# Alternating the two head halves of the Gram products, and grouping attention scores by term, in a two-layer trunk step

## The chip, the cores and the metric

The kernel runs on one core of a Trainium2 chip. The metric is the device time of one execution in microseconds. The kernel before takes 3819.39 us (median of 3 runs, 3814.24 to 3825.59). The engines of the core are named as in the profile: PE is the matmul engine (TensorE), PEld its weight loads, DVE VectorE, ACT ScalarE, POOL GpSimd, and SP the engine that issues the DMAs.

## The reference

One inference step of a two-layer trunk over 128 context tokens and 512 latent tokens, width 2048, all in float32. Every layer is a modulated RMSNorm, a mixer, and a gated residual.

Layer 0 has eight differential-attention heads and eight multi-head-latent-attention (MLA) heads. A latent query reads 512 latent keys and 256 context keys in one softmax; a context query reads the 128 context keys. What matters here is the scores:

```python
# differential head, for each of its two score maps c
s = einsum('bqhcd,bkhcd->bhcqk', q, k_all) * 64 ** -0.5
# MLA head: two products are added
s = (einsum('bqhd,bkhd->bhqk', qn, k_nope) + einsum('bqhd,bkd->bhqk', qp, kpe_all)) * 192 ** -0.5
```

Layer 1 is a bidirectional RWKV-7 scan over 32 heads of width 64:

```python
sa = einsum('bhij,bhj->bhi', s, -kk_t)
s = s * w_t[:, :, None, :] + sa[..., None] * (kk_t * a_t)[:, :, None, :] + v_t[..., None] * k_t[:, :, None, :]
y_t = einsum('bhij,bhj->bhi', s, r_t)
```

The outputs are both token streams after a final RMSNorm, the new caches and the new scan states.

## The kernel before, in words

Activations lie transposed, with the channels on the partitions and the 640 tokens along the free axis. The large projections run in `project_steps` (L111): a weight chunk is split into a high part (ACT, L100) and a low part (POOL, L101), and each product is taken as three matmuls of 320 columns per token half (L126, tile `pj`). One step of this generator is one pair of matmuls. TensorE's program order is written out by hand: around every small piece of attention or scan the program calls `fill(w)`, which issues `w` times a quota of projection steps. The other engines' order comes from a scheduler with priorities.

**Attention scores (`scores`, L370).** For 128 queries the keys stand in one or two segments: 512 latent keys and 256 context keys for latent queries, one segment of 128 for context queries. Scores are a sum of terms. In a differential head there are two: a stacked high-precision product with 128 rows (`KA`), and a low-order correction that reads only the 64 partitions of its own score map (`KL`). In an MLA head there are three: the 128-row product (`kn`), the rope product with 128 rows (`kpeh`), and its correction with 64 rows (`kpel`). The two segments go to two PSUM banks of one tile `S`. The loop takes the segments one after the other, and all terms inside a segment. `S` has one buffer; DVE's maximum (L362) and ACT's exponential (L365) read it before the next scores may be written.

**The scan.** It runs in 32 units, two for each tile of 128 channels, and a tile holds two heads: head half 0 on partitions 0 to 63, half 1 on 64 to 127. A unit covers ten chunks of 64 tokens. The stages of several units overlap: while `stage_c` of unit n steps through the recurrence, earlier stages prepare the units n + 1 and n + 2. After `stage_c`, the list `P2` says in which order the rest of the preparation is done and how much projection work follows each step. `stage_a2` (L1104) of unit n + 2 is last in that list.

`stage_a2` makes the Gram products: for every chunk and each head half one fp32 matmul with 64 rows, 128 stationary columns and 128 moving columns (L1114), `BK` against `AR`. Four chunks of one half fill one PSUM bank, and DVE multiplies the bank with the triangular mask into `GG` (L1117). The PSUM pool `pg` that these banks come from has two buffers, which the stages `a1`, `kk`, `bk`, `pre`, `gn` and `bonus` use too. The stage is a generator with six steps: chunks 0 to 3 of half 0, then of half 1, chunks 4 to 7 of each, chunks 8 and 9 of each. `stage_a3` later sends `GG` through a DRAM buffer (`Ld`) and inverts its diagonal blocks; `stage_c` and `stage_pre` read `GG` as well.

Of the kernel before, what the change touches and what calls it, by code (L numbers as in the profile page):

```python
# [53 lines left out]
def kernel(  # L54
# [189 lines left out]
    with tc.tile_pool(name="x0", bufs=1, side="right") as xp0, \  # L244
# [11 lines left out]
        pss = [pt[:, 512 - HT:512], pt[:, 512:512 + HT]]  # L256
# [63 lines left out]
    with l0:  # L320
# [47 lines left out]
            return P, r  # L368

        def scores(S, terms, qa, segs):  # L370
            so = 0
            for (ka, kb) in segs:
                for i, (q, k) in enumerate(terms):
                    pe.matmul(S[:, so:so + kb - ka], q[:, qa:qa + 128], k[:, ka:kb],  # L374
                              start=(i == 0), stop=(i == len(terms) - 1))
                so += kb - ka

        def stack_q(QA, q, c):
            me, ot = slice(64 * c, 64 * c + 64), slice(64 - 64 * c, 128 - 64 * c)
# [151 lines left out]
        def s_part(H, t):  # L531
            qa, segs, kts = QT[t]
            n = 128 * len(kts)
            for c, terms in enumerate(H.terms):
                S = pS.tile([128, 1024], F32, tag="S", name="S")
                scores(S, terms, qa, segs)
                with tc.high_priority(offset=HP0):
                    P, r = softmax(S, n, f"P{c}", pools["dif"] if c else at)
                    if c == 0:
                        H.P = P  # L540
                        dve.tensor_scalar(out=P[:, 0:n], in0=P[:, 0:n], scalar1=r, scalar2=None, op0=ALU.mult)
                    else:
                        dve.tensor_tensor(out=r, in0=r, in1=nlam, op=ALU.mult)
                        dve.scalar_tensor_tensor(out=H.P[:, 0:n], in0=P[:, 0:n], scalar=r, in1=H.P[:, 0:n],
                                                 op0=ALU.mult, op1=ALU.add)
                yield
# [50 lines left out]
        def fill(w):  # L597
            quota[0] += w * quota[1]
            while quota[0] >= 1.0:
                quota[0] -= 1.0  # L600
                next(work[0], None)
# [236 lines left out]
    with ExitStack() as l1:  # L838
# [39 lines left out]
        def pg_tile(name):  # L878
            return pg.tile([128, 512], F32, tag="pg", name=name)
# [116 lines left out]
        def need(f, i):  # L996
            while i < 16 and (f, i) not in done:
                next(work[0])
# [105 lines left out]
        def stage_a2(i, u):  # L1104
            un = units[(i, u)]
            AR, BK = un.AR, un.BK
            GG = un.GG = u1.tile([128, NCH, 2, 128], F32, tag="GG", name="GG", bufs=2)
            for c in range(0, NCH, 4):
                n = min(4, NCH - c)
                for h in range(2):  # L1110
                    hs = slice(64 * h, 64 * h + 64)
                    ps = pg_tile("gram")
                    for j in range(n):
                        pe.matmul(ps[:, j * 128:(j + 1) * 128],  # L1114
                                  BK[hs, c + j, :, :].rearrange("p a t -> p (a t)"),
                                  AR[hs, c + j, :, :].rearrange("p a t -> p (a t)"), start=True, stop=True)
                    dve.tensor_tensor(  # L1117
                        out=GG[:, c:c + n, h, :], in0=ps[:, 0:n * 128].rearrange("p (j t) -> p j t", t=128),
                        in1=maskg.rearrange("p (o t) -> p o t", o=1).to_broadcast([128, n, 128]), op=ALU.mult)
                    yield  # L1120

        def stage_a3(i, u):
            un = units[(i, u)]
# [328 lines left out]
        def kk_of(n):  # L1452
            if n < len(seq) and seq[n][1] == 0:
                return stage_kk(seq[n][0])
            return iter(())

        def of(stage, n):
            return stage(*seq[n]) if n < len(seq) else iter(())

        def all_(*gens):  # L1460
            for g in gens:
                for _ in g:
                    pass

        def urgent(g):
            while True:
                with tc.high_priority(offset=HP):
                    try:
                        v = next(g)
                    except StopIteration:  # L1470
                        return
                yield v
# [8 lines left out]
                next(work[0], None)  # L1481

        CW = (3, 3, 2, 3)
        P2 = (('inv', 1), ('bk', 2), ('inv', 2), ('bk', 1), ('pre', 2), ('inv', 2), ('bonus', 1), ('bk', 1), ('inv', 2), ('pre', 2), ('bonus', 2), ('pre', 2), ('pre', 2), ('a2', 0), ('a2', 2), ('a2', 1), ('a2', 2), ('a2', 1), ('a2', 4))
        W2 = sum(w for _, w in P2)

        def step(g):
            next(g, None)

        def unit(n):  # L1490
# [23 lines left out]
            all_(sub, a1, gn, kk, of(stage_e, n + 2))  # L1514
            quota[1] = max(0.0, (total - w1) / W2)
            gens = dict(inv=inv, bk=of(stage_bk, n + 1), a2=of(stage_a2, n + 2), pre=of(stage_pre, n + 1), bonus=bonus)
            for k, w in P2:
                step(gens[k])
# [3 lines left out]
        def script(gens, items):  # L1522
            for k, w in items:
                step(gens[k])
                fill(w)
            all_(*gens.values())

        def prologue():
            quota[1] = 1.0
            need(proj_k, 0)  # L1530
            script(dict(kk=kk_of(0), a1=of(stage_a1, 0)),
                   (("a1", 9), ("a1", 9), ("kk", 9), ("kk", 7), ("a1", 7), ("kk", 5), ("a1", 0)))
            need(proj_r, 0)
            all_(of(stage_e, 0))
            fill(36)
            a1, bk = of(stage_a1, 1), of(stage_bk, 0)
            a2 = of(stage_a2, 0)
            for g, w in ((a2, 2), (a2, 2), (a1, 6), (a2, 2), (a2, 2), (a1, 6), (a2, 2), (a2, 2)):
                step(g)
                fill(w)  # L1540
            all_(a2, of(stage_a3, 0))
            for g, w in ((bk, 6), (bk, 6), (a1, 8), (bk, 6)):
                step(g)
                fill(w)
            all_(a1, bk)
            need(proj_v, 0)
            all_(of(stage_e, 1))
            of(stage_v, 0)
            script(dict(pre=of(stage_pre, 0), inv=urgent(of(stage_inv, 0)), a2=of(stage_a2, 1)),
                   (("pre", 6), ("pre", 32), ("inv", 3), ("a2", 3), ("inv", 3), ("a2", 3), ("a2", 3), ("inv", 3),  # L1550
                    ("a2", 3), ("pre", 3), ("inv", 3), ("a2", 3), ("pre", 3), ("a2", 3)))
            need(proj_r, 1)

        with tc.manual_schedule(engines={mybir.EngineType.PE}):
            prologue()
            for n in range(30):
                unit(n)
            unit(30)
            e2.release()
            ysp.append(tc.alloc_tile_pool(name="ysp", bufs=2, side="right"))  # L1560
            free_slots()
            unit(31)
            pc.release()
            pj3 = ctx.enter_context(tc.tile_pool(name="pj3", bufs=1, space=PSUM))
            gn = stage_gn(15, 1)
            step(gn)
            all_(work[0])
            all_(gn)
            stage_end(15, 1)
            y1_tile(15)  # L1570
            begun.append(out_begin(2, pj3, w_o1, y1hi, y1lo, 0))
            all_(interleaved([begun[2][1]], 3))
# [119 lines left out]
```

## Time and profile before

| what | before |
|---|---|
| median of 3 runs | 3819.39 us (3814.24 to 3825.59) |
| profiled execution | 3822.71 us, of which its span is 3820.9 us |
| mean granted TensorE clock | 0.979 |
| PE busy | 3607.5 us, 34176 matmul passes |
| DVE, ACT, POOL busy | 2203.8, 1607.6, 1193.5 us |
| MLA heads | about 230 to 625 us |
| differential heads | about 640 to 1280 us |
| Gram products (L1114) | 1628.6 to 3492.5 us, 1280 passes, 183.8 us busy |

The span runs from the first to the last instruction of the profiled execution. An fp32 matmul stands in the trace as two passes, each with a weight load (PEld) of its own; a matmul on the rounded type of the projections is one pass. A row gives an instruction's start, duration, engine, line, operation, and output and inputs by name; `64*128 64x128` means 64 rows and 128 stationary columns, and 64 partitions by 128 moving columns. The ends of matmuls are modelled and overlap the next one, so distances between starts say more than durations. "idle before" is the time in which the engine had nothing running ahead of a group, with what ended it.

### The profile page before, as it was taken

What the parts mean: (1) busy time and instruction counts of PE and PEld (TensorE: products, weight loads), DVE (VectorE), ACT (ScalarE), POOL (GpSimd) and SP (SyncE); (2) the same over time, 40 slices, a digit from 0 to 9 for tenths busy, and PEclk for the clock granted to TensorE, in tenths of its full rate; (3) what the DMA queues carried; (4) which work ended last, traced back from release to release, by engine and by line L of the source; (5) the groups of instructions that cost most, each with busy time, mean ns of one, the idle gap of its engine ahead of it and who ended that gap; (6) DMA issues with size and microseconds to landing.
All of it is one profiled execution on the core that took longest, in us unless ns stands there. A gap on an engine that the chain in (4) does not pass through costs nothing. (4 is left out here: it accounts for less than half of the span.)

```text
span 3820.9 us, 83259 instructions
## 1 busy us (share of the span) xinstructions
PE 3607.5 (94%) x34176; PEld 3121.5 (82%) x34176; DVE 2203.8 (58%) x4232; ACT 1607.6 (42%) x3310; POOL 1193.5 (31%) x1094
## 2 busy tenths in 40 slices
PE   8999999999999899999999999999999999999998
PEld 4778889888888798888777878878878787787898
DVE  3346655666567683555666566656666666666402
ACT  3244443444444323534444444434444444445422
POOL 1222122222222345433232232323323332232444
PEclk9999999999999999989999999999999999999999
DMA  8723333333334464322222222222222222223534
GB/s 296 233 68 106 113 91 109 104 101 106 104 103 131 147 206 142 91 64 56 71 60 62 59 61 71 60 62 57 66 69 60 67 59 65 67 65 85 164 99 141
DMA packets 388462, 376.18 MB, mean 98 GB/s; under 512 B 200496, under 2 KB 242416, under 8 KB 388080
## 3 DMA queue, kind: packets, MB, share of 16 engines
q1 hardware_dynamic: 388080, 370.86, 33.5%
q8 instruction: 268, 4.39, 0.5%
q14 instruction: 114, 0.93, 0.1%
HBM read 328.51 MB, written 42.24 MB: 97 GB/s over the span
## 5 line engine op out<-in xcount | busy, mean ns | idle before, releaser
L101 POOL TENSOR_TENSOR wlo<-raw,whi 128x512 fp32r<-128x512 f32 (+1 forms) x628 | 854.9, 1362 | 2164.9 <-PE pj L126 1303.2
L126 PE MATMUL pj<-h0hi,wlo 128*128 128x320 f32 x4448 | 1092.5, 324 | 18.7 <-POOL wlo L101 18.7
L126 PE MATMUL pj<-h0hi,whi 128*128 128x320 f32 x4448 | 1091.5, 324 | 4.5 <-DVE gt L951 3.1
L126 PE MATMUL pj<-h0lo,whi 128*128 128x320 f32 x4448 | 1083.8, 323 | 2.0 <-DVE h0lo L816 1.2
L126 PEld LDWEIGHTS pj<-h0hi,wlo 128*128 128x128 f32 x4448 | 748.0, 191 | 53.9 <-POOL wlo L101 22.4
L126 PEld LDWEIGHTS pj<-h0hi,whi 128*128 128x128 f32 x4448 | 747.7, 192 | 37.9 <-ACT whi L100 3.9
L126 PEld LDWEIGHTS pj<-h0lo,whi 128*128 128x128 f32 x4448 | 751.2, 191 | 29.4 <-DVE h0lo L816 1.5
L100 ACT ACTIVATE whi<-raw 128x512 fp32r<-128x512 f32 (+1 forms) x628 | 390.7, 623 | 793.0 <-PE pj L126 491.5
L198 DVE SCALAR_TENSOR_TENSOR aacc<-araw,scs,aacc 128x512 f32<-128x512 f32 x480 | 405.2, 892 | 17.8 <-DMA araw<-in_dram 16.8
L362 DVE TENSOR_REDUCE nm<-S 128x1 f32<-128x768 f32 (+1 forms) x120 | 98.4, 820 | 280.6 <-PE S L374 280.5
L1117 DVE TENSOR_TENSOR GG<-gram,con 128x512 f32<-128x512 f32 (+1 forms) x192 | 113.6, 599 | 145.2 <-PE gram L1114 144.2
L1114 PE MATMUL gram<-AR,BK 64*128 64x128 f32 x1280 | 183.8, 293 | 10.4 <-DVE GG L1117 5.2
L1114 PEld LDWEIGHTS gram<-AR,BK 64*128 64x128 f32 x1280 | 151.3, 192 | 44.2 <-issue 20.1
L722 DVE SCALAR_TENSOR_TENSOR x<-pj,mod,xr 128x512 f32<-128x512 f32 (+2 forms) x68 | 33.2, 524 | 248.7 <-PE pj L126 243.2
L365 ACT ACTIVATE P<-S,nm 128x768 f32<-128x768 f32 (+1 forms) x120 | 95.0, 792 | 175.7 <-DVE nm L362 175.5
L1302 ACT ACTIVATE Yn<-CC 128x128 f32<-128x128 f32 x160 | 44.3, 277 | 224.1 <-DVE rhs L1332 213.4
L1347 DVE COPY UV<-CC 64x128 f32<-64x128 f32 x160 | 47.1, 295 | 124.7 <-ACT UV L1346 123.1
L1054 PE MATMUL plo<-lr,lw 96*128 96x320 f32 x256 | 104.0, 488 | 6.6 <-DMA lr<-lorad 6.4
L1346 ACT ACTIVATE UV<-CC 64x128 f32<-64x128 f32 x160 | 43.1, 269 | 150.2 <-PE CC L1344 149.7
L564 PE MATMUL po<-PT,vt 128*128 128x128 f32 x800 | 103.2, 276 | 0.1
L564 PEld LDWEIGHTS po<-PT,vt 128*128 128x128 f32 x800 | 97.9, 191 | 4.2 <-issue 2.5
L1056 ACT ACTIVATE tmp<-plo,vecs 128x320 f32<-128x320 f32 x128 | 67.5, 527 | 66.1 <-PE plo L1054 66.0
(338 smaller groups left out, 5401.1 us busy)
## 6 DMA issues: line engine op xcount, KB each, us to landing
raw<-in_dram SPq DMA_DIRECT2D x612, 256.0 KB
araw<-in_dram SPq DMA_DIRECT2D x384, 256.0 KB
lr<-lorad SPq DMA_DIRECT2D x128, 120.0 KB
Ld<-GG SPq DMA_DIRECT2D x64, 160.0 KB
lw<-in_dram SPq DMA_DIRECT2D x128, 48.0 KB
x<-in_dram SPq DMA_DIRECT2D x16, 320.0 KB
xr<-in_dram SPq DMA_DIRECT2D x16, 320.0 KB
DD<-Xd SPq DMA_DIRECT2D x32, 160.0 KB
```

Of the source, the lines that this page charges most:

```text
L100: act.activation(out=hi, in_=src, func=AF.Copy)
L101: (lo_eng or pool).tensor_tensor(out=lo, in0=src, in1=rf(hi), op=ALU.subtract)
L126: pe.matmul(p[:n, 0:b - a], w, x[:, kk ^ flip, a:b], start=(kk == order[0] and i == 0), stop=(kk == order[-1] + kc - 1 and i == 2))
L198: dve.scalar_tensor_tensor(out=acc[:, s], in0=raw, scalar=scs[:, k, s:s + 1], in1=acc[:, s], op0=ALU.mult, op1=ALU.add)
L362: dve.tensor_reduce(out=nm, in_=S[:, 0:nk], axis=AX.X, op=ALU.max, negate=True)
L365: act.activation(out=P[:, 0:nk], in_=S[:, 0:nk], func=AF.Exp, bias=nm, accum_out=l)
L564: pe.matmul(po[:, 0:128], H.vt[:, kt, :], PT[:, j, :], start=(j == 0), stop=(j == n - 1))
L1054: pe.matmul(ps[:, 0:HT], lw, lo, start=True, stop=True)
L1056: act.activation(out=hv(tmp, z, ca, cb), in_=c3(ps[:, 0:HT]), func=AF.Exp, scale=-1.0, bias=nw0[:, bcol:bcol + 1])
L1114: pe.matmul(ps[:, j * 128:(j + 1) * 128], BK[hs, c + j, :, :].rearrange("p a t -> p (a t)"), AR[hs, c + j, :, :].rearrange("p a t -> p (a ...
L1117: dve.tensor_tensor(out=GG[:, c:c + n, h, :], in0=ps[:, 0:n * 128].rearrange("p (j t) -> p j t", t=128), in1=maskg.rearrange("p (o t) -> p ...
L1347: dve.tensor_copy(out=UV[64:128, cgs[1], :], in_=pu[1][64:128])
```

## The change

Three things are edited. In `scores` the two loops change places: the outer loop runs over the terms and the inner one over the key segments. In `stage_a2` both banks are taken at once, the matmuls of the two head halves alternate between them, and both masked copies follow; the generator has three steps instead of six. The three lists that call its steps are rewritten for three steps, with the same total of fill weights.

```diff
         def scores(S, terms, qa, segs):
-            so = 0
-            for (ka, kb) in segs:
-                for i, (q, k) in enumerate(terms):
+            for i, (q, k) in enumerate(terms):
+                so = 0
+                for ka, kb in segs:
                     pe.matmul(S[:, so:so + kb - ka], q[:, qa:qa + 128], k[:, ka:kb],
                               start=(i == 0), stop=(i == len(terms) - 1))
-                so += kb - ka
+                    so += kb - ka
...
             for c in range(0, NCH, 4):
                 n = min(4, NCH - c)
-                for h in range(2):
-                    hs = slice(64 * h, 64 * h + 64)
-                    ps = pg_tile("gram")
-                    for j in range(n):
+                pss = [pg_tile("gram") for _ in range(2)]
+                for j in range(n):
+                    for h, ps in enumerate(pss):
+                        hs = slice(64 * h, 64 * h + 64)
                         pe.matmul(ps[:, j * 128:(j + 1) * 128],
                                   BK[hs, c + j, :, :].rearrange("p a t -> p (a t)"),
                                   AR[hs, c + j, :, :].rearrange("p a t -> p (a t)"), start=True, stop=True)
+                for h, ps in enumerate(pss):
                     dve.tensor_tensor(
                         out=GG[:, c:c + n, h, :], in0=ps[:, 0:n * 128].rearrange("p (j t) -> p j t", t=128),
                         in1=maskg.rearrange("p (o t) -> p o t", o=1).to_broadcast([128, n, 128]), op=ALU.mult)
-                    yield
+                yield
...
-        P2 = (('inv', 1), ('bk', 2), ('inv', 2), ('bk', 1), ('pre', 2), ('inv', 2), ('bonus', 1), ('bk', 1), ('inv', 2), ('pre', 2), ('bonus', 2), ('pre', 2), ('pre', 2), ('a2', 0), ('a2', 2), ('a2', 1), ('a2', 2), ('a2', 1), ('a2', 4))
+        P2 = (('inv', 1), ('bk', 2), ('inv', 2), ('bk', 1), ('pre', 2), ('inv', 2), ('bonus', 1), ('bk', 1), ('inv', 2), ('pre', 2), ('bonus', 2), ('pre', 2), ('pre', 2), ('a2', 3), ('a2', 3), ('a2', 4))
...
-            for g, w in ((a2, 2), (a2, 2), (a1, 6), (a2, 2), (a2, 2), (a1, 6), (a2, 2), (a2, 2)):
+            for g, w in ((a2, 4), (a1, 6), (a2, 4), (a1, 6), (a2, 4)):
...
-                   (("pre", 6), ("pre", 32), ("inv", 3), ("a2", 3), ("inv", 3), ("a2", 3), ("a2", 3), ("inv", 3),
-                    ("a2", 3), ("pre", 3), ("inv", 3), ("a2", 3), ("pre", 3), ("a2", 3)))
+                   (("pre", 6), ("pre", 32), ("inv", 3), ("a2", 6), ("inv", 3), ("inv", 3),
+                    ("a2", 6), ("pre", 3), ("inv", 3), ("pre", 3), ("a2", 6)))
```

TensorE's program order in a differential head, for 128 latent queries and one score map (S is the score tile, QA the queries, KA and KL the keys' 128-row and 64-row terms). Before:

```order
L374 MATMUL S<-KA,QA 128x512
L374 MATMUL S<-KL,QA 128x512
L374 MATMUL S<-KA,QA 128x256
L374 MATMUL S<-KL,QA 128x256
L126 MATMUL pj<-h0hi,wlo 128x320 x2
```

Now:

```order
L374 MATMUL S<-KA,QA 128x512
L374 MATMUL S<-KA,QA 128x256
L374 MATMUL S<-KL,QA 128x512
L374 MATMUL S<-KL,QA 128x256
L126 MATMUL pj<-h0hi,wlo 128x320 x2
```

The two 128-row products now stand together, and the two 64-row ones. Next, TensorE's program order in the Gram stage of one unit late in the scan (the numbers tell buffers apart: each gram number is one PSUM bank filling). Before:

```order
L1114 MATMUL gram_34687<-AR_34392,BK_34393 128x128 x4
L1114 MATMUL gram_34693<-AR_34392,BK_34393 128x128 x4
L126 MATMUL pj_34296<-h0hi_95,whi_34638 128x320 x2
L126 MATMUL pj_34296<-h0lo_96,whi_34638 128x320 x2
L126 MATMUL pj_34296<-h0hi_95,wlo_34639 128x320 x2
L1114 MATMUL gram_34705<-AR_34392,BK_34393 128x128 x4
L126 MATMUL pj_34739<-h0hi_95,whi_34741 128x320 x2
L1114 MATMUL gram_34748<-AR_34392,BK_34393 128x128 x4
```

Now:

```order
L1114 MATMUL gram_34687<-AR_34392,BK_34393 128x128
L1114 MATMUL gram_34688<-AR_34392,BK_34393 128x128
L1114 MATMUL gram_34687<-AR_34392,BK_34393 128x128
L1114 MATMUL gram_34688<-AR_34392,BK_34393 128x128
...
L126 MATMUL pj_34296<-h0hi_95,whi_34638 128x320 x2
L126 MATMUL pj_34296<-h0lo_96,whi_34638 128x320 x2
L126 MATMUL pj_34296<-h0hi_95,wlo_34639 128x320 x2
L126 MATMUL pj_34733<-h0hi_95,whi_34735 128x320 x2
L1114 MATMUL gram_34742<-AR_34392,BK_34393 128x128
L1114 MATMUL gram_34743<-AR_34392,BK_34393 128x128
```

Matmuls of the two halves alternate between two banks, and four projection steps stand between the first visit and the second, which again takes both banks. In all but the two units of the prologue four or five steps stand there. Last, DVE's order in the same unit (GG is the masked copy, gt a gate tile of the projection, Yn the scan's output). Before:

```order
L1402 TENSOR_TENSOR Yn<-Yn,gst 128x640
L1117 TENSOR_TENSOR GG<-gram,con 128x4x128 x2
L946 SCALAR_TENSOR_TENSOR gt<-pj,vecs,gt 128x319
L1117 TENSOR_TENSOR GG<-gram,con 128x4x128
L946 SCALAR_TENSOR_TENSOR gt<-pj,vecs,gt 128x320
L1117 TENSOR_TENSOR GG<-gram,con 128x4x128
L1117 TENSOR_TENSOR GG<-gram,con 128x2x128
```

Now:

```order
L1403 TENSOR_TENSOR Yn<-Yn,gst 128x640
L1118 TENSOR_TENSOR GG<-gram,con 128x4x128 x2
L946 SCALAR_TENSOR_TENSOR gt<-pj,vecs,gt 128x319
L946 SCALAR_TENSOR_TENSOR gt<-pj,vecs,gt 128x320
L1118 TENSOR_TENSOR GG<-gram,con 128x4x128 x2
L951 TENSOR_TENSOR gt<-gt,pj 128x160
L1118 TENSOR_TENSOR GG<-gram,con 128x2x128
```

The copies of a visit now stand in pairs, and the Yn product stands in front of the first pair as before. From L1114 on, the changed kernel's line numbers are up to one higher.

## The prediction

> **What bounds the kernel now.** I read the page's first part, then the busy time of three stretches, then who waits for whom in the scan.
>
> ```profile
> PE 3607.5 (94%) x34176; PEld 3121.5 (82%) x34176; DVE 2203.8 (58%) x4232; ACT 1607.6 (42%) x3310; POOL 1193.5 (31%) x1094
> ...
> 230.00:625.00 395.00, 387.48 (x2339) 327.59 (x2338) 219.53 (x333) 163.14 (x334) 79.79 (x64) 1.00 0.32 98
> 640.00:1280.00 640.00, 626.63 (x3908) 557.77 (x3908) 401.80 (x621) 282.83 (x544) 176.61 (x124) 0.99 0.35 105
> ...
> 1628.00:3495.00 1867.00, 1755.78 (x22233) 1493.23 (x22233) 1176.11 (x2612) 847.71 (x1856) 573.43 (x639) 0.97 0.25 64
> ```
>
> The columns of a stretch are its length, then the busy time of PE, PEld, DVE, ACT and POOL, the granted clock, and DMA. In the MLA heads (230 to 625) and the differential heads (640 to 1280) TensorE is busy 98% of the time, in the scan (1628 to 3495) 94%; no other engine passes 63%. So a microsecond off TensorE's queue is nearly a microsecond off the end, unless TensorE then waits for an engine that was late anyway. Those waits in the scan, longest first:
>
> ```profile
> PE CC L1264 <- ACT xd L1258: 31.3, 28, 2.6
> PE CC L1344 <- ACT Yn L1302: 14.2, 29, 0.8
> PE CC L1298 <- DVE S L1369: 14.0, 22, 1.6
> PE CC L1354 <- DVE UV L1347: 12.2, 16, 1.1
> ...
> PE gram L1114 <- DVE GG L1117: 5.2, 6, 1.4
> ...
> DVE GG L1117 <- PE gram L1114: 144.2, 125, 7.2
> ```
>
> TensorE's four largest waits come to 72 us of 1867. At the Gram products the wait goes the other way: DVE stands idle 144.2 us for them. So this is a place where TensorE is late.
>
> **The Gram products.** One unit's Gram stage on TensorE as it is now (start, duration, row; each x count is of passes, two per fp32 matmul):
>
> ```profile
> 3187.39 0.45 PE L126 MATMUL pj<-h0hi,wlo 128*128 128x320 f32 x2
> 3187.78 1.71 PE L1114 MATMUL gram<-AR,BK 64*128 64x128 f32 x16
> 3189.42 0.56 PE L126 MATMUL pj<-h0hi,whi 128*128 128x320 f32 x2
> 3189.82 0.46 PE L126 MATMUL pj<-h0lo,whi 128*128 128x320 f32 x2
> 3190.11 0.46 PE L126 MATMUL pj<-h0hi,wlo 128*128 128x320 f32 x2
> 3190.49 1.16 PE L1114 MATMUL gram<-AR,BK 64*128 64x128 f32 x8
> 3191.58 0.56 PE L126 MATMUL pj<-h0hi,whi 128*128 128x320 f32 x2
> 3192.07 1.16 PE L1114 MATMUL gram<-AR,BK 64*128 64x128 f32 x8
> 3193.16 0.56 PE L126 MATMUL pj<-h0lo,whi 128*128 128x320 f32 x2
> ...
> 3194.23 0.71 PE L1114 MATMUL gram<-AR,BK 64*128 64x128 f32 x4
> 3194.87 0.56 PE L126 MATMUL pj<-h0lo,whi 128*128 128x320 f32 x2
> ...
> 3195.65 0.71 PE L1114 MATMUL gram<-AR,BK 64*128 64x128 f32 x4
> 3196.29 0.56 PE L126 MATMUL pj<-h0hi,whi 128*128 128x320 f32 x2
> ```
>
> From a Gram group's start to the next projection matmul: 1.64 us for 16 passes, 1.09 for 8, 0.64 for 4. One half's passes therefore cost (1.09 - 0.64) / 4 = 0.1125 us each. Going in and out costs more: the pair before takes 0.39 us (3187.39 to 3187.78), the pair after 0.40 (3189.42 to 3189.82), an undisturbed pair 0.29, so 0.21 us per visit. A unit now pays 1.64 + 2 x 1.09 + 2 x 0.64 + 5 x 0.21 = 6.15 us.
>
> The 16-pass row is the key. It is half 0's eight passes and then half 1's eight, with nothing between. Serially it would take 1.09 + 8 x 0.1125 = 1.99 us; it took 1.64. Three passes' worth ran at once where the halves met, although they read different partitions of the same arrays and write different banks. So two 64-row products do run side by side. How completely, if they alternate throughout, a row of small products that already alternates shows:
>
> ```profile
> 3184.18 1.15 PE L1217 MATMUL pmv<-UV,GG 64*64 64x64 f32 x32
> 3185.26 0.56 PE L126 MATMUL pj<-h0hi,whi 128*128 128x320 f32 x2
> ...
> 3186.33 0.45 PE L1217 MATMUL pmv<-UV,GG 64*64 64x64 f32 x8
> 3186.71 0.56 PE L126 MATMUL pj<-h0hi,whi 128*128 128x320 f32 x2
> ```
>
> Its 24 further passes cost 1.08 - 0.38 = 0.70 us, 0.029 each; half of a Gram pass (64 columns, not 128) is 0.056. That is 1.93 at a time. A pair of alternating Gram passes then takes about 2 x 0.1125 / 1.93 = 0.117 us, so a visit of 16 passes 1.09 + 8 x 0.004 = 1.12 us and one of 8 passes 0.66. A changed unit pays 2 x 1.12 + 0.66 + 3 x 0.21 = 3.53 us: 2.62 less. Thirty units look like the one above. The first two, in the prologue, have six visits, 4 x 1.09 + 2 x 0.64 + 6 x 0.21 = 6.90 us, and save 3.37. Sum: 30 x 2.62 + 2 x 3.37 = **85 us**. If alternating overlapped no more than the 16-pass row does (0.35 us a visit), a unit would pay 2 x 1.85 + 0.95 = 4.65 and the sum would be 50 us; that is the lower bound. The upper is 88 (no loss from pairing: 1.09 and 0.64 a visit). The weights that share out the projection between the visits still come to 10 a unit, so no projection pass moves to another unit; the last copies of GG come earlier too, so the chain that starts from them (the Ld transfer) is not late.
>
> **What the Gram change adds.** Each visit now fills both banks, so the next visit needs both masked copies done, where before it needed only the older one. The copies, in this unit and on average:
>
> ```profile
> 3188.97 1.29 DVE L1117 TENSOR_TENSOR GG<-gram,con 128x512 f32<-128x512 f32 x2 [0.56 <-PE gram L1114]
> ...
> L1117 DVE TENSOR_TENSOR GG<-gram,con 128x512 f32<-128x512 f32 x128 | 86.6, 687 | 84.7 <-PE gram L1114 83.8
> L1402 DVE TENSOR_TENSOR Yn<-Yn,gst 128x640 f32<-128x640 f32 x32 | 33.9, 1060 | 9.6 <-ACT gst L1401 9.6
> ...
> L1114 PEld LDWEIGHTS gram<-AR,BK 64*128 64x128 f32 x1280 | 151.3, 192 | 44.2 <-issue 20.1 <-DVE GG L1117 13.1 <-ACT MV L1219 5.6
> ```
>
> Both are through 3190.26 - 3187.78 = 2.48 us after a visit starts. In the new order four or five projection steps (0.29 us each) stand between visits, so TensorE is back after 1.12 + 0.21 + 4 x 0.29 = 2.49 us: a tie, and 0.29 us to spare with five. Where DVE has something like the Yn product (1.06 us) in front, TensorE waits, and behind it wait the projection and the next unit's first step. The same holds at the first visit for the last MV copy on ACT, which half 1 needs now almost at once. I put +8 us on the 44.2 us of today, of which 162 visits x 0.19 = 31 are the bare change of mode (30 units x 5 and 2 x 6). The bounds are 0 and 32 us (half a 1 us operation at each of the 64 second and third visits).
>
> **The scores.** One pair of key segments in a differential head:
>
> ```profile
> 802.30 0.40 PE L374 MATMUL S<-KA,QA 128*128 128x512 f32 x1
> 802.63 0.50 PE L374 MATMUL S<-KL,QA 64*128 64x512 f32 x1
> 803.06 0.38 PE L374 MATMUL S<-KA,QA 128*128 128x256 f32 x1
> 803.37 0.38 PE L374 MATMUL S<-KL,QA 64*128 64x256 f32 x1
> 803.68 0.56 PE L126 MATMUL pj<-h0hi,wlo 128*128 128x320 f32 x2
> ...
> L374 PE MATMUL S<-KL,QA x144: 322/381/792, 640.1 to 1276.8; 64*128 64x512 f32 x64, 64*128 64x256 f32 x64, 64*128 64x128 f32 x16
> L374 PE MATMUL S<-kpel,QA x72: 322/383/502, 234.2 to 623.0; 64*128 64x512 f32 x32, 64*128 64x256 f32 x32, 64*128 64x128 f32 x8
> ```
>
> The steps are 0.33, 0.43, 0.31 and 0.31 us. A 512 and a 256 column step that both follow a change between 128 and 64 rows differ by 0.12 us, so 256 columns cost 0.12, 512 cost 0.24, and the change itself 0.19 to 0.20. The order now makes four changes (128, 64, 128, 64, back to 128); grouped by term there are two. Two fewer save 0.40 us; 0.38 to 0.43 by the rows. There are 64 such groups in the differential heads and 32 in the MLA heads, where the low-order rope term is the one with 64 rows; the 24 groups with one segment stay as they are. 96 x 0.40 = **38 us**. No DMA or other engine moves: the softmax starts when the last matmul of the group is done, as before.
>
> That rests on the weight load of the 256-column matmul hiding behind the 512-column one on the same rows. It could fail: the first step, a change whose load falls into the next step, has only 0.33 - 0.24 = 0.09 us over its columns, so the drain is 0.09 and the load the other 0.10. If the load stayed visible, a change removed would save 0.09 us, and the scores 96 x 0.18 = 17 us. The projection pairs speak for hiding: 2 x 320 columns at 0.12 us per 256 are 0.30 us of streaming, and a pair takes 0.29. The Trainium skill (TensorE: Matmul & The Clock Gate, Part 3, What overlaps and what doesn't) says that a weight load overlaps a running matmul only where the row group differs, which would mean the 17; the projection rows don't agree with it.
>
> **The sum**, on the profiled execution's own 3822.7 us: -85 - 38 + 8, and +12 for other waits in the scan that grow when TensorE arrives earlier (a tenth of the 123; bounds 0 and a third). That gives 3719.7. The profiled execution was 3.3 us over the median of the runs, so I predict **3716 us**, 2.7% less.
>
> **The rivals.**
> 1. The products don't run at once and the change doesn't do what it says. Then a visit costs 1.99 + 0.21, a small one 1.09 + 0.21, a unit 5.70: 16 us saved in all, and 3822.7 - 16 + 8 - 38 + 5 = 3782, 3778 on the median. Against it stands the 16-pass row, which could not take 1.64 us.
> 2. The scan is held by its chains of several engines, and two thirds of the 85 us turn into waits at CC, like those listed: 3822.7 - 28 - 38 = 3757, 3753. For it: 94% and not 98% busy, and a different engine behind nearly every wait. Against it: the listed waits are short, and DVE waits for TensorE at the very place that gets faster.
> 3. Slower: evacuation decides. If DVE's order puts an operation of about 1.06 us in front of each of the two copies, the second and third visit of each unit wait 2.1 us: 64 x 2.1 = 134 us, and 3822.7 - 123 + 12 + 134 = 3846, 3842. It decides from a mean wait of 1.75 us on (112 / 64). Against it: the copies of a unit take 4 x 0.687 + 2 x 0.424 = 3.6 us of DVE, and TensorE spends 3.53 + 9 x 0.29 = 6.1 there. The Trainium skill (TensorEngine Tiling (Array Packing), PSUM Bottleneck) warns that after a speed-up by tiling the PSUM copy may become the bottleneck; that is this rival, and no row shows it yet.
> 4. The load of the second segment stays visible: the scores give 17 us and not 38, 3737. Against it, the projection pairs.
>
> ```profile
> L1117 DVE TENSOR_TENSOR GG<-gram,con 128x256 f32<-128x256 f32 x64 | 27.1, 424 | 60.5 <-PE gram L1114 60.4
> ```
>
> **How the numbers follow.** Forecast 0.68, rival 1 0.08, rival 2 0.13, rival 4 0.04; rival 3 0.04, and 0.03 for waits of about 1.6 to 1.9 us, which cancel the gain. About 0.3% (11.5 us) is what a measurement can tell from no change. Faster 0.93, same 0.03, slower 0.04. The forecast's own range is 3690 (no added waits, pairing without loss, 0.43 us a score group: 3822.7 - 88 - 41 - 3.3) to 3748 (Gram at its lower bound, 3822.7 - 50 - 38 + 8 + 9 - 3.3); rival 2 with a few us of its own takes the high end to 3765, and rivals 1 and 3 are left out.
>
> **What would show it.** Right: Gram busy time on TensorE falls from 183.8 us to near 100; a 16-pass visit takes 1.1 to 1.2 us to the next projection; score groups lose 0.40 us; gram's wait for GG stays under 30 us. Wrong: a 16-pass visit near 2 us (rival 1); the CC waits of the scan grow by tens of us (rival 2); gram waits for GG over 60 us (rival 3); the 256-column score step behind its own term takes 0.22 us or more instead of about 0.12 (rival 4).

## The result, and the profile after

| | before | with the change |
|---|---|---|
| median | 3822.49 us (4 runs) | 3716.23 us (4 runs, 3702.09 to 3723.01) |
| ratio, 95% interval | | 0.9701 (0.9671 to 0.9731) |
| profiled execution | 3822.71 us | 3717.45 us, span 3715.7 |
| mean granted TensorE clock | 0.979 | 0.980 |

The change is faster by 3.0%, and 3716 us had been predicted. The total is right. Several of its terms are not, and they cancel; the busy times show where to look.

First part of the page of the changed kernel, then the same stretches as before the change: MLA heads, differential heads, and scan (length, then busy time of PE, PEld, DVE, ACT and POOL, granted clock, DMA):

```profile
PE 3491.8 (94%) x34176; PEld 3054.6 (82%) x34176; DVE 2183.1 (59%) x4232; ACT 1608.9 (43%) x3310; POOL 1189.5 (32%) x1094
```

```profile
237.00:615.00 378.00, 369.67 (x2303) 322.91 (x2302) 215.58 (x328) 161.58 (x330) 80.38 (x63) 1.00 0.33 100
632.00:1255.00 623.00, 601.79 (x3893) 549.44 (x3892) 401.71 (x618) 283.10 (x543) 176.64 (x124) 0.99 0.35 107
1608.00:3385.00 1777.00, 1667.85 (x22220) 1422.70 (x22221) 1156.04 (x2612) 849.58 (x1856) 570.74 (x638) 0.98 0.27 67
```

Before, cut at the same instructions:

```profile
233.00:623.00 390.00, 382.48 (x2304) 322.73 (x2302) 217.48 (x329) 161.64 (x330) 79.05 (x63) 1.00 0.32 98
639.00:1277.00 638.00, 624.63 (x3893) 555.59 (x3891) 400.06 (x617) 282.84 (x543) 176.18 (x124) 0.99 0.35 105
1628.00:3493.00 1865.00, 1753.78 (x22218) 1491.49 (x22219) 1174.56 (x2609) 847.71 (x1856) 572.56 (x639) 0.97 0.25 64
```

The MLA heads give 12 us and the differential heads 15, together 27 where 38 were predicted. The scan gives 88 where 85 - 8 - 12 = 65 were predicted. The rest of the program, in which nothing was edited, is 10 us longer.

One Gram unit of the changed kernel, TensorE by time:

```profile
3202.16 1.16 PE L1114 MATMUL gram<-AR,BK 64*128 64x128 f32 x16
3203.25 0.56 PE L126 MATMUL pj<-h0hi,whi 128*128 128x320 f32 x2
...
3204.61 1.24 PE L1114 MATMUL gram<-AR,BK 64*128 64x128 f32 x16
3205.78 0.56 PE L126 MATMUL pj<-h0lo,whi 128*128 128x320 f32 x2
...
3207.44 0.71 PE L1114 MATMUL gram<-AR,BK 64*128 64x128 f32 x8
3208.08 0.55 PE L126 MATMUL pj<-h0hi,whi 128*128 128x320 f32 x2
```

From start to next projection row the visits take 1.09, 1.17 and 0.64 us. Sixteen alternating passes take as long as eight of one half did before, so pairing costs nothing. The second visit's 0.08 us more is a wait, and DVE's rows show for what:

```profile
3203.35 1.29 DVE L1118 TENSOR_TENSOR GG<-gram,con 128x512 f32<-128x512 f32 x2 [0.74 <-PE gram L1114]
```

The copies end at 3204.64, 2.48 us after the visit began, and TensorE is back at 3204.61: the tie that the prediction spoke of. For the whole scan, the idle time in front of the Gram operations by what ended it (us, times), first before the change, then after:

```profile
  DVE GG L1117: 18.3, 42
  ACT MV L1219: 7.8, 19
```

```profile
  DVE GG L1118: 37.9, 61
  ACT MV L1220: 11.6, 30
```

TensorE and its loads now stand 19.6 us longer for the masked copies. Such a figure adds the idle time of the matmuls and that of the weight loads (5.2 and 13.1 us before, 13.8 and 24.1 after), so one wait can stand in it twice; how far the queue itself was held up is worked out from starts further below. TensorE's longest waits in the scan:

```profile
PE CC L1265 <- ACT xd L1259: 27.2, 25, 2.6
PE CC L1345 <- ACT Yn L1303: 17.5, 37, 0.8
PE gram L1114 <- DVE GG L1118: 13.8, 18, 3.4
PE CC L1355 <- DVE UV L1348: 12.4, 16, 1.1
...
PE CC L1299 <- DVE S L1370: 9.1, 24, 0.8
```

The four waits at CC that the prediction quoted came to 71.7 us; they are 66.2 now. They did not grow.

A score group of a differential head now:

```profile
788.98 0.51 PE L374 MATMUL S<-KA,QA 128*128 128x512 f32 x2
789.42 0.61 PE L374 MATMUL S<-KL,QA 64*128 64x512 f32 x2
789.96 0.56 PE L126 MATMUL pj<-h0hi,wlo 128*128 128x320 f32 x2
```

It takes 0.98 us to the next projection row instead of 1.38: 0.40 us less, as predicted. The two passes of 768 columns on the same rows take 0.44 us with part of the change to 64 rows; the second weight load does not show.

### The profile page after: what moved, and what is told of

It is laid out like the page before. It is cut to its first block, busy times and chain, and to the rows that moved or that the text cites. A ratio compares the mean times of both kernels' runs of the same rounds, so it can differ in the third digit from the quotient of the medians.

```text
span 3715.7 us, 83258 instructions
## 1 busy us (share of the span) xinstructions
PE 3491.8 (94%) x34176; PEld 3054.6 (82%) x34176; DVE 2183.1 (59%) x4232; ACT 1608.9 (43%) x3310; POOL 1189.5 (32%) x1094
## 5 line engine op out<-in xcount | busy, mean ns | idle before, releaser
L1114 PE MATMUL gram<-AR,BK 64*128 64x128 f32 x1280 | 115.9, 295 | 20.8 <-DVE GG L1118 13.8
L1114 PEld LDWEIGHTS gram<-AR,BK 64*128 64x128 f32 x1280 | 91.8, 191 | 46.3 <-DVE GG L1118 24.1
```

The costliest lines, as they stand in the source:

```text
L1114: pe.matmul(ps[:, j * 128:(j + 1) * 128], BK[hs, c + j, :, :].rearrange("p a t -> p (a t)"), AR[hs, c + j, :, :].rearrange("p a t -> p (a ...
```

## The experiments

The theory: both edits gain on TensorE what the rows say, and the scan gives part of it back at the masked copies. The rivals concern the alternation (is it only the halved number of visits?), the row-mode change (is it the price in the scores?), and the wait for the copies (can it be had back, and can it eat the gain?). Every ratio below is against the kernel before, run on the same chip.

### Each edit alone, and the change once more

The first kernel has the changed Gram products with the score loop of before. The second has the score loop alone; its diff against the kernel before is:

```diff
-            so = 0
-            for (ka, kb) in segs:
-                for i, (q, k) in enumerate(terms):
+            for i, (q, k) in enumerate(terms):
+                so = 0
+                for ka, kb in segs:
```

> Only the Gram stage is changed; the scores are as before. Theory (two 64-row products run side by side, three visits instead of five): the visits are worth 88 us of TensorE, and the trace of the changed kernel shows 20 us more waiting for the masked copies than before, so 65 to 80 us less than before, ratio 0.979 to 0.983. If the two edits take gain from each other (TensorE faster in one place waits in the other), the two single edits together give clearly more than the 106 us of both.

> Only the order of the scores is changed; the Gram stage is as before. Theory: 96 groups lose two changes of row mode each, 38 us of TensorE; of this the trace of the changed kernel gives 10 us back as longer waits elsewhere in the heads, so 27 us less than before, ratio 0.993. If those 10 us are the scatter of one execution, 38 us, ratio 0.990.

> The changed kernel once more, beside the runs of the kernel before on this chip. If the two edits simply add, its ratio is the product of the two single ones, 0.9805 x 0.9944 = 0.975 (about 95 us less than before); if the first measurement of 0.970 stands, the two together give some 18 us more than singly.

| | median | ratio |
|---|---|---|
| Gram products alone | 3754.33 us (5 runs) | 0.9805 (0.9779 to 0.9831) |
| scores alone | 3804.50 us (7 runs) | 0.9944 (0.9922 to 0.9967) |
| the change again | 3719.77 us (5 runs) | 0.9719 (0.9692 to 0.9747) |

Alone, the Gram products give 75 us (0.0195 x 3827) and the scores 21. The product of the two ratios is 0.975; the change itself measured 0.970 and 0.972. That is inside what the intervals leave open: nothing here speaks against edits that simply add. The scores give 21 us, with about 8 us either way: that agrees with the 27 us in the trace of the whole change and not with 38.

### The banks without the alternation

Both banks, three visits and both copies behind each visit stay; only the loops change places, so that half 0's products all come before half 1's.

```diff
-                for j in range(n):
-                    for h, ps in enumerate(pss):
+                for h, ps in enumerate(pss):
+                    for j in range(n):
```

> The changed kernel with three visits and both banks at once, but all matmuls of half 0 first and then all of half 1. Theory (alternating is what makes them run side by side): a 16-pass visit goes back to 1.64 us, a small one to about 0.74, which is 64 x 0.55 + 32 x 0.10 = 38 us slower than the changed kernel: about 3754 us, ratio 0.982 to before. Rival (fewer visits and the paired copies are what counts): within 8 us of the changed kernel, ratio 0.970.

3742.69 us (4 runs), ratio 0.9783 (0.9755 to 0.9812). TensorE in one unit:

```profile
3229.08 1.71 PE L1114 MATMUL gram<-AR,BK 64*128 64x128 f32 x16
3230.72 0.56 PE L126 MATMUL pj<-h0hi,whi 128*128 128x320 f32 x2
...
3235.39 0.72 PE L1114 MATMUL gram<-AR,BK 64*128 64x128 f32 x8
3236.04 0.55 PE L126 MATMUL pj<-h0hi,whi 128*128 128x320 f32 x2
```

A 16-pass visit takes 1.64 us grouped and 1.09 alternating, with the same number of visits and the same banks. Sixty-four of them make 35 us; the measured ratios are apart by 0.006 to 0.008, 24 to 31 us. So the alternation is a gain of its own beside the smaller number of visits. The two numbers are not the same microseconds, though. The idle time in front of the Gram operations in this kernel:

```profile
  DVE GG L1118: 10.7, 16
```

That was 37.9 us (61 times) with the alternation: a longer visit leaves DVE more time for the copies. Added up from the starts of TensorE's matmuls in the profiled execution, and with half clock taken out, the Gram stage costs about 10 us more here than with the change, and the recurrence (CC) 10 us more; TensorE stood at half clock in the scan for 89 us, against 68 with the change and 77 when the change was run again. Why the recurrence is slower was not found. The 8-pass visits hardly differ (0.65 and 0.64 us), which the expectation had priced too high: where only four passes follow four, nearly all of the second half runs beside the first.

### The 64-row correction padded to 128 rows

The low-order terms of the scores read all 128 partitions instead of 64. This adds a product of two low-order parts, which the kernel before leaves out.

```diff
-            H.terms = [((qn, kn), (QA, kpes[0]), (QA[me], kpes[1][me]))]
+            H.terms = [((qn, kn), (QA, kpes[0]), (QA, kpes[1]))]
...
-            H.terms = [((QA[:, c], KA[:, c]), (QA[64 * c:64 * c + 64, c], KL[64 * c:64 * c + 64])) for c in range(2)]
+            H.terms = [((QA[:, c], KA[:, c]), (QA[:, c], KL)) for c in range(2)]
```

> The changed kernel, with the correction term of the scores taken over all 128 partitions instead of 64. In the MLA heads the other 64 rows add the product of the two low-order parts; in the differential heads they add a product of two low-order parts that belong to different score maps, of the size of the rounding. No change of row mode is left in the scores. Theory (the mode change costs 0.2 us): two more changes go from each of 96 + 24 groups, 48 us of TensorE, of which about 10 come back as waits: about 3680 us, ratio 0.962 to before. Rival (what counted was that the two segments of one term stand together, for instance that a weight load is shared or hidden): as the changed kernel, 0.970.

3685.95 us (4 runs), ratio 0.9635 (0.9608 to 0.9662). A score group of this kernel:

```profile
793.70 0.51 PE L374 MATMUL S<-KA,QA 128*128 128x512 f32 x2
794.04 0.51 PE L374 MATMUL S<-KL,QA 128*128 128x512 f32 x2
794.39 0.46 PE L126 MATMUL pj<-h0lo,whi 128*128 128x320 f32 x2
```

It takes 0.69 us instead of 0.98. The columns are the same; what went is the change from 128 to 64 rows and back. A part of it lies in the projection pair behind the group. The next pair's row, with the change and then here:

```profile
790.35 0.45 PE L126 MATMUL pj<-h0hi,whi 128*128 128x320 f32 x2
```

```profile
794.68 0.45 PE L126 MATMUL pj<-h0hi,wlo 128*128 128x320 f32 x2
```

The pair behind the group takes 0.39 us (789.96 to 790.35) with the change and 0.29 here. So the change of row count is the price, 0.29 + 0.10 us for two, the 0.19 to 0.20 each that the prediction had, and the regrouping of the loops could only halve it. Added up over the 120 groups and the pairs behind them, 45 us went from TensorE's queue.

Not all of it arrives at the end. The heads as a whole are 32 us shorter than with the change in the profiled executions. The idle time of TensorE and its loads in front of the scores, until ACT's exponential had read the score tile, in this kernel:

```profile
  ACT P L365: 37.9, 19
```

Before the change this was 14.9 us (11 times), with it 24.2 (14 times). The longest of these waits, TensorE and DVE of the padded kernel by time:

```profile
782.01 1.01 PE L374 MATMUL S<-KA,QA 128*128 128x512 f32 x2 [3.98 <-ACT P L365]
...
783.46 0.73 PE L126 MATMUL pj<-h0hi,whi 128*128 128x320 f32 x2
783.99 0.73 PE L126 MATMUL pj<-h0lo,whi 128*128 128x320 f32 x2
```

```profile
774.31 5.76 DVE L198 SCALAR_TENSOR_TENSOR aacc<-araw,scs,aacc 128x512 f32<-128x512 f32 x7
779.99 0.94 DVE L362 TENSOR_REDUCE nm<-S 128x1 f32<-128x768 f32 x1
```

DVE's maximum, which the exponential needs, stands behind seven sums of the modulation (5.76 us). The score tile has one buffer, so TensorE waits for the exponential, and all projection work queued behind the next scores waits with it. Faster scores reach that wait earlier. The second thing to see is the pace afterwards: the projection pairs follow each other by 0.53 us, not 0.29. That is the granted clock, and more of it follows.

### More and less projection work between the Gram visits

The three visits of a unit stand in the list `P2` with the projection work that follows each. The first kernel moves work from behind the last visit to the places between, the second does the opposite; the total stays ten.

```diff
-('a2', 3), ('a2', 3), ('a2', 4))
+('a2', 5), ('a2', 5), ('a2', 0))
```

```diff
-('a2', 3), ('a2', 3), ('a2', 4))
+('a2', 0), ('a2', 0), ('a2', 10))
```

> The changed kernel with the projection weights behind the three Gram visits 5, 5, 0 in place of 3, 3, 4: seven or eight projection steps between visits instead of four or five, and none behind the last. Theory (what is left at the Gram visits is the wait for the two masked copies, 30 us in the trace at second and third visits): some 20 us less than the changed kernel, ratio 0.965. Rival (the wait comes from DVE being late at this place anyway, and the steps taken away behind the last visit are missed in the next unit's first recurrence step): no change, 0.970, or slower.

> The changed kernel with weights 0, 0, 10: the three Gram visits stand back to back. Theory (a visit needs both copies of the one before, which are through 2.48 us after that visit's start, while the visit itself takes 1.12 us): every second and third visit waits about 1.3 us, 64 x 1.3 = 83 us, of which 30 are there already: 50 us slower than the changed kernel, about 3766 us, ratio 0.985 to before. Rival (DVE is not behind; the copies hide): as the changed kernel.

| | median | ratio |
|---|---|---|
| 5, 5, 0 | 3690.55 us (5 runs) | 0.9634 (0.9606 to 0.9661) |
| 0, 0, 10 | 3867.26 us (4 runs) | 1.0101 (1.0071 to 1.0131) |

Idle time in front of the Gram operations, of 5, 5, 0 and then of 0, 0, 10:

```profile
  ACT MV L1220: 18.0, 39
  DVE GG L1118: 14.2, 23
```

```profile
  DVE GG L1118: 143.1, 176
```

With more work between the visits the wait for the copies falls from 37.9 to 14.2 us, and the kernel gains 29 us over the change measured beside it (3719.77), where 20 had been expected. The wait of the first visit for ACT's last MV copy grows by 6 us. Not all of the 29 us is waiting. With no projection behind the last visit, the 64-row products of the recurrence (L1326) follow it directly in 30 units, so two changes of row count fall away in each: at 0.19 us some 11 us, an estimate. With none between the visits, the wait is 143.1 us (58.5 in front of matmuls, 84.7 in front of their loads), and the kernel is slower than before the change. The prediction's third rival is a real mechanism, then; four or five projection steps are what keeps it small.

The second kernel lost far more than expected: 147 us over the change where 50 had been written down. A unit of it, TensorE by time:

```profile
2176.10 1.16 PE L1114 MATMUL gram<-AR,BK 64*128 64x128 f32 x16
2178.89 0.57 PE L1114 MATMUL gram<-AR,BK 64*128 64x128 f32 x2 [1.63 <-DVE GG L1118]
2179.75 2.07 PE L1114 MATMUL gram<-AR,BK 64*128 64x128 f32 x14 [0.28 <-DVE GG L1118]
2182.20 1.81 PE L1114 MATMUL gram<-AR,BK 64*128 64x128 f32 x8 [0.37 <-DVE GG L1118]
2183.94 0.90 PE L126 MATMUL pj<-h0hi,wlo 128*128 128x320 f32 x2
```

And the busy times of this kernel in the 4 us with the wait and the 4 us behind them, with the granted clock third from the end:

```profile
2175.00:2179.00 4.00, 2.37 (x27) 1.96 (x23) 3.67 (x7) 1.42 (x3) 2.35 (x3) 1.00 0.09 28
2179.00:2183.00 4.00, 3.35 (x20) 2.67 (x22) 1.98 (x4) 0.00 (x0) 0.00 (x0) 0.52 0.12 37
```

TensorE was busy for 2.37 of 4 us; in the next 4 us its clock is 0.52, and a visit that takes 0.64 us elsewhere takes 1.74. So the wait is paid twice here, first as idle time and then as slow work. The whole execution ran at a clock of 0.957 against 0.980 with the change. Read as time at half clock that is 0.023 / 0.5 x 3870 = 178 us more, and work at half clock loses nearly half of it: 80 to 90 us. The other 57 to 67 us are near the 50 that had been expected from the wait itself, but that is partly luck: 30 units now have one visit in place of three, and the 120 changes of row count that they lose are worth some 23 us by the same estimate, so the waits cost more than 50. This split is worked out, not measured apart.

### Different shares of work in the heads

The padded kernel with the forward shares of the differential heads' projection work shifted, to put more in front of the second scores:

```diff
-        FW = ((0.09, 0.06, 0.58, 0.27), (0.12, 0.35, 0.28, 0.25))
+        FW = ((0.09, 0.06, 0.58, 0.27), (0.10, 0.45, 0.25, 0.20))
```

> The kernel with full-row scores (e4), and in the differential heads more projection work between the two score maps: the four shares of the fill become 0.10, 0.45, 0.25, 0.20 in place of 0.12, 0.35, 0.28, 0.25. Theory (what came back of the scores' gain is the second map's scores waiting until the first map's softmax has read the one score tile, because DVE's maximum stands behind adaLN sums; 19 us before scores in the trace of e4): 10 us less than e4, about 3675 us, ratio 0.961. Rival (the waits move to the transposes behind the softmax): no change, 0.9635.

3698.13 us (5 runs), ratio 0.9661 (0.9634 to 0.9689): no better than the padded kernel. Idle time in front of the scores, and then in front of the transposes of the softmax's result:

```profile
  ACT P L365: 5.5, 4
```

```profile
  DVE P L544: 29.0, 16
```

The wait for the exponential fell from 37.9 to 5.5 us, and the wait for DVE's scaled result rose from 10.8 to 29.0. The waiting was only moved. What is late is DVE's chain, by these two waits. Whether another place for the modulation sums, or a second score buffer, would remove the wait was not tried.

### The two gains together

The first kernel is the padded scores with 5, 5, 0. The second also moves two parts of work ahead of the first Gram visit, where 5, 5, 0 waits for ACT's MV copy:

```diff
-('pre', 2), ('pre', 2), ('a2', 5), ('a2', 5), ('a2', 0))
+('pre', 2), ('pre', 4), ('a2', 4), ('a2', 4), ('a2', 0))
```

> Full-row scores (e4) and Gram weights 5, 5, 0 (e5) together. They lie in different stages of the program, so if both readings hold they add: 0.9635 + 0.9634 - 0.9719 = 0.955, about 3654 to 3665 us. If TensorE's earlier arrival were taken back further on, nearer 0.962.

> As e9, but two of the ten weights stand in front of the first Gram visit, where ACT's copy of MV (18 us of waiting in the trace of e5) must leave the second bank: the last step of that copy has 4, and the visits 4, 4, 0. Theory (the first visit waits for MV because half 1 needs its bank at once): some 8 us less than e9, ratio 0.953. Rival (the steps between the visits are worth more, since the tie with the masked copies comes back nearer): as e9 or up to 8 us more.

| | median | ratio |
|---|---|---|
| padded scores with 5, 5, 0 | 3650.65 us (5 runs) | 0.9563 (0.9534 to 0.9591) |
| 4, 4, 0 with two parts ahead | 3639.87 us (4 runs) | 0.9529 (0.9501 to 0.9558) |

Idle time in front of the Gram operations, of the second:

```profile
  DVE GG L1118: 18.0, 29
...
  ACT MV L1220: 1.8, 7
```

The wait for MV fell from 17.8 to 1.8 us, and the copies' wait rose by 3. The last kernel is 4.7% under the kernel before and about 1.9% under the change. Both steps did what was expected; the intervals of these two overlap, so the last step alone is not proved by its times.

## Why the prediction was right, point by point

**What bounds the kernel.** Right. TensorE is still busy 94% of the span, and what left its queue left the end, except at the places below.

**The Gram products, 85 us.** Right. Visits of 1.12 and 0.66 us were predicted from the row of small products that alternated already; 1.09 and 0.64 were measured without a wait, the no-loss bound, so 88 us and not 85 before the waits. (The small products alternate between output halves too, so this was an extrapolation; it held.) The first rival (no overlap) falls by the same rows, and the kernel without the alternation shows that the overlap comes from the order of the passes. One sign was set wrongly: busy time of Gram fell from 183.8 to 115.9 us, not near 100, since many visits hold a wait inside them: from start to next projection row all visits take 115.5 us, and without waits they would take 64 x 1.09 + 32 x 0.64 = 90.

**"I put +8 us" for both copies.** Too small. The wait for GG grew by 19.6 us by the rows of matmuls and loads, inside the bounds of 0 and 32. The starts of TensorE's matmuls, where nothing counts twice, say about the same: in the scan the Gram stage and the projection pairs around it take 62 us less than before when half of the time at half clock is taken out, where 88 without added waits would have come, so some 26 us were lost at the copies of GG and MV. The tie was seen, but the value chosen for it was nearly that of no wait. Moving work between the visits took 23.7 us off the rows' figure again. The third rival's sign (over 60 us) did not come; its mechanism did when the work between the visits was taken out.

**"+12 for other waits in the scan".** Wrong in sign: the four quoted waits shrank by 5.5 us, and by the starts the recurrence (CC) took 10 us less, so the second rival falls too. Why it took less was not found. At full clock that is 62 + 10 = 72 us, and the scan gave 88. The rest is the granted clock. By the clock records TensorE stood at half clock in the scan for 102 us before and 69 after, and at the loss of about half this is the missing 17. Outside heads and scan it went the other way, from 46 to 66 us, which is the 10 us by which the unedited rest grew; in the heads it was 10 and 14. The whole program has 159 and 149 us, some 5 us of time. So most of this is a matter of where the slow stretches fell in the two profiled executions, and not a gain of the change.

**The scores, 38 us.** The mechanism and the price of a group are right: 0.40 us measured, and without any change of row count another 0.29 and 0.10 in the pair behind. Over all groups 37 us went. The fourth rival falls, as the weight load behind a 512-column matmul on the same rows does not show: in the padded kernel 768 columns take 0.34 us (793.70 to 794.04), and the prediction's 0.12 us for 256 columns gives 0.36. The Trainium skill (TensorE: Matmul & The Clock Gate, Part 3, What overlaps and what doesn't), by which a load overlaps only where the row group differs, does not agree with these rows. What failed is the sentence "No DMA or other engine moves: the softmax starts when the last matmul of the group is done, as before". It starts earlier by 0.40 us only where DVE is free, and the longest wait of the padded kernel shows DVE in the middle of other sums. The wait in front of the scores grew from 14.9 to 24.2 us, and that in front of the transposes for DVE's result from 2.7 to 7.8, by the rows that add matmuls and loads. By starts TensorE lost 5 us in front of the scores, 5 at the transposes and 1 to the clock, nearly all in the differential heads: the MLA heads gave 12 of their 13 us, the differential heads 15 of 26. So 27 us arrived in the trace, and 21 in the times of the score loop alone. The prediction put TensorE's waits in the scan into its sum and none in the heads, where a busy share of 98% seemed to leave no room.

**The total.** The scores gave 11 us less than predicted and the Gram stage 15 less (62 in place of 85 - 8), the other work of the scan 22 more (10 gained in place of 12 lost), and the clock 5 more: these cancel. The two edits work as predicted, but that the total came out within a microsecond is luck, and the four runs alone lie 21 us apart.

## What to carry to other kernels

Products of 64 rows that stand on opposite partition halves and write different banks should alternate pass by pass; put enough other work between two fillings of the same banks: with none, the wait for the evacuation cost more here than the overlap gained. A 64-row term between 128-row terms pays for the change each way, so group such terms, and pad them to 128 rows where the small extra products are harmless. When TensorE is nearly always busy, look in the trace for what the next engine does at the moment when the faster result arrives: its queue, not its busy share, decides how much of the gain is kept.

## What the runs showed of the hardware

**Half clock can follow short waits.** In the changed kernel, too, half clock follows a stretch in which TensorE is idle for about a third of 4 us, with no long wait in it. The rows of one such stretch, then its busy times and those of the 4 us behind it:

```profile
3112.28 0.34 PE L1299 MATMUL CC<-S,AR 64*64 64x64 f32 x8 [0.45 <-DVE S L1370]
3113.45 0.33 PE L1326 MATMUL CC<-S,AR 64*64 64x64 f32 x4 [0.82 <-DVE S L1372]
```

```profile
3111.00:3115.00 4.00, 2.74 (x31) 2.09 (x31) 2.65 (x5) 1.87 (x5) 1.27 (x1) 0.99 0.29 45
3115.00:3119.00 4.00, 4.00 (x34) 3.09 (x30) 0.29 (x1) 0.80 (x2) 0.44 (x2) 0.58 0.42 106
```

Waits of 0.45 and 0.82 us leave TensorE busy for 2.74 of 4 us, and for the next 4 us the clock is 0.58. The Trainium skill (TensorE: Matmul & The Clock Gate, Part 1, HAM oscillation) gives idle gaps of more than about 3.4 us as what brings the slow clock; a later section of that part (A second HAM failure mode) tells of short idle times between groups that do it as well, and these rows agree with the second. It is not a rule that could be used for a forecast: in the same trace TensorE is busy for only 2.28 us between 2788 and 2792, and the 4 us behind have full clock (1.00).

**The scatter between runs goes with this clock.** Of the kernel before, in the runs beside the first experiments, the fastest (3810.75 us) had a clock of 0.985 and one of the slowest (3838.58 us) 0.974. Time at half clock differs by 0.011 / 0.5 x 3820 = 84 us between them, and 28 us of time go with it. Which of the two drives the other is not shown, as a wait can bring half clock and half clock makes work late.

**A second 64-row product, alternating with the first, cost nothing more.** Sixteen passes of two halves took the 1.09 us of eight passes of one. Grouped by half they took 1.64.
